# Two-layer transformer block on one core: the layer norm between the last two attentions computed with tokens on partitions, two convolution blocks read where they were accumulated, and the last two token blocks of the output left to VectorE

## The chip, the cores and the metric

The kernel runs on one core of a Trainium2 chip. The core has TensorE (PE in the rows), VectorE (DVE), ScalarE (ACT), GpSimd (POOL), a queue engine that issues transfers (SP), and 16 DMA engines. The metric is the device time of one execution in microseconds (us).

## The reference

x has 512 tokens of 1024 channels. A first block mixes a causal depthwise convolution (width 31) with a dilated window attention and is followed by a feed-forward layer. A second block has two more attentions, and after each of them a residual and a layer norm. The parts that the change touches:

```python
a = a_val * jax.nn.sigmoid(a_gate)
a = causal_depthwise_conv(a, conv_w[l], conv_b[l])
a = jax.nn.silu(rms_norm(a, conv_norm_g[l]))
y_a = a @ w_conv_out[l]
...
def layer_norm(x, g, b):
    mu = jnp.mean(x, axis=-1, keepdims=True)
    var = jnp.mean(jnp.square(x - mu), axis=-1, keepdims=True)
    return (x - mu) * lax.rsqrt(var + LN_EPS) * g + b
...
for i in range(DEPTH_2):                    # i = 0: dsa_mixer, i = 1: stick_breaking_mixer
    y = mixer(x, ...)                       # ends in (o * silu(g)) @ w_out
    x = layer_norm(ALPHA * x + y, ln_g[i], ln_b[i])
```

## The kernel before

Activations lie with channels on partitions: a [1024, 512] matrix is 8 tiles ("blocks", c = 0 to 7) of 128 channels by 512 tokens. Every fp32 product is made of three matmuls on halves of the operands, `hi*hi`, `hi*lo` and `lo*hi` (lines 302 to 304, always in that order); a pair `h, l` of tiles such as `Ah, Al` is such a split, made by ScalarE (`h`) and VectorE (`l`). The class `Weights` loads 512 KB weight blocks (`wraw`, two in flight), ScalarE rounds them to `whi` (line 120) and GpSimd subtracts to get `wlo` (line 124).

TensorE's order is written out by hand: `Stream` holds a list of chunks (one chunk is the three matmuls of one of a product's 8 input blocks), `pe.after(n, fn)` runs `fn` when n more chunks are issued, and `together` takes chunks of several products in turn. The other engines' instructions are put in order by a scheduler.

The places that the change touches:

1. **The convolution's end (stage `mid1`).** Each convolution block is accumulated by VectorE. Six of the eight blocks are done earlier; blocks 6 and 7 (`LATE`) run here, each in a PSUM bank of tag `pt`, while TensorE multiplies by `w_attn_out`. When the last tap is done, ScalarE copies the bank to SBUF (line 834) and squares the copy (line 1016); the sum of squares goes through `ones_d` on TensorE at a fixed place (`pe.pull(YB)`, lines 1031 and 1032), and ScalarE forms `rc` = exp(-0.5 ln) (lines 1034 and 1035, shown as L193 in the rows). VectorE then works on the 8 blocks (lines 1039, 1042, 1045) and also drains the banks of the `w_attn_out` products (line 1025); the products with `w_conv_out` come next and need both.
2. **The layer norm between the two attentions (class `Between`).** The products with `w_out_a` (class `Outward`) come as six whole blocks and two blocks in token halves (`TS`, 256 tokens each). Means and variances are sums over partitions: VectorE and GpSimd add up blocks, `ones_h` and `ones_d` on TensorE sum over partitions, in `middle` (a provisional mean of blocks 0 to 3) and in `stats` (once for each half). `stats` then normalizes 8 blocks with VectorE, GpSimd and ScalarE. Three products of the next layer's gates (`AHEAD`) follow in halves, then the next layer's query block.
3. **The output (class `Last`)** has the tokens on partitions already: `turn` transposes each finished block on TensorE (line 1315) into `pt` banks, ScalarE copies them to `y`, VectorE takes `bn_stats`; `finish` normalizes two token blocks at a time. Token block 1 is done by ScalarE and GpSimd (`APART`), block 3 half by them and half by VectorE, blocks 0 and 2 by VectorE.

## Time and profile before

| | us |
|---|---|
| median of 3 runs (1580.19 to 1585.54) | 1583.32 |
| profiled execution | 1582.75 |
| its span, first to last instruction | 1580.9 |
| TensorE busy | 1519.2 |
| VectorE busy | 1133.5 |
| ScalarE busy | 827.1 |
| GpSimd busy | 767.0 |

The profile is of one execution, 1.85 us longer than its span and 0.57 us under the median. Busy time is a sum over the span; pipelined matmuls overlap, so a busy TensorE isn't one at its peak. In a timeline row the columns are start (us), duration (us), engine, line, operation, output<-input, operand shapes, count, and in brackets the idle time ahead of it and what is taken to have ended it.

### The profile page before, as it was taken

The page shows a single profiled execution, that of the slowest core. Times are in us where ns is not written, and L with a number is a line of the kernel's source. Part 1 is how long each engine was busy: PE and PEld are TensorE (multiplying, and loading weights), DVE is VectorE, ACT ScalarE, POOL GpSimd, SP SyncE. Part 2 cuts the span into 40 slices and gives each one's busy share as a digit, 9 for nine tenths or more (in the row PEclk, how much of TensorE's full clock was granted, in tenths as well). Part 3 has the DMA queues.
Part 4 walks back from the last instruction along what each step waited for, and adds up shares of the span by engine and source line. Part 5 has one row for each costly group of instructions (what it writes and reads, how often), then busy time and mean ns, then how long its engine had stood idle before and what let it go on. Part 6 is the DMA issues. An engine that isn't in the chain of part 4 may idle for free.

```text
span 1580.9 us, 21344 instructions
## 1 busy us (share of the span) xinstructions
PE 1519.2 (96%) x7870; PEld 1290.7 (82%) x7870; DVE 1133.5 (72%) x1867; ACT 827.1 (52%) x1495; POOL 767.0 (49%) x650
## 2 busy tenths in 40 slices
PE   7999999998999999999999989999999789999996
PEld 5888888887878888888888878888887678888885
DVE  8996578777867567627726679988887765777764
ACT  4454678777343443424424344376665445666642
POOL 3687533333735644454454464544552875334324
PEclk9999999999999999999999999999999799999998
DMA  4333321211324333243332342322220313212212
GB/s 142 91 107 93 107 68 41 80 54 54 98 75 119 108 93 89 85 120 94 93 107 87 95 121 68 93 57 78 62 59 14 95 53 94 68 54 81 67 54 80
DMA packets 234604, 130.37 MB, mean 82 GB/s; under 512 B 5206, under 2 KB 232774, under 8 KB 234500
## 3 DMA queue, kind: packets, MB, share of 16 engines
q1 hardware_dynamic: 234356, 128.75, 27.9%
q8 instruction: 62, 1.02, 0.3%
q14 instruction: 42, 0.34, 0.1%
q10 hardware_dynamic: 144, 0.26, 0.0%
HBM read 126.90 MB, written 2.10 MB: 82 GB/s over the span
## 4 chain that ended last, share of the span: by engine, by line
PE 57%; DVE 25%; ACT 8%; issue 4%; POOL 3%; DMA 3%; SPq 0%; DVEq 0%; ACTq 0%; POOLq 0%
PE pj L302 9%; PE pj L303 9%; PE pj L304 9%; DVE pt L832 6%; PE s L303 5%; PE s L302 5%; PE s L304 5%; PE o L513 3%; POOL wlo L124 2%; PE pt L594 2%; PE pj L326 2%; PE pj L328 2%; PE pj L327 2%; PE s L583 1%; DVE score L1445 1%
## 5 line engine op out<-in xcount | busy, mean ns | idle before, releaser
L124 POOL TENSOR_TENSOR wlo<-wraw,whi 128x256 fp32r<-128x256 f32 (+2 forms) x548 | 654.2, 1218 | 698.7 <-ACT whi L120 655.0
L120 ACT CAST whi<-wraw 128x1024 fp32r<-128x1024 f32 (+3 forms) x255 | 243.9, 965 | 243.9 <-PE pj L303 79.0
L302 PE MATMUL pj<-Ah,whi 128*128 128x512 f32 (+3 forms) x896 | 359.5, 401 | 3.7 <-DVE v L719 2.1
L304 PE MATMUL pj<-Ah,wlo 128*128 128x512 f32 (+3 forms) x896 | 348.3, 389 | 2.8 <-POOL wlo L124 2.8
L303 PE MATMUL pj<-Al,whi 128*128 128x512 f32 (+3 forms) x896 | 348.5, 389 | 0.0
L304 PEld LDWEIGHTS pj<-Ah,wlo 128*128 128x128 f32 (+1 forms) x896 | 168.9, 189 | 39.2 <-POOL wlo L124 4.1
L302 PEld LDWEIGHTS pj<-Ah,whi 128*128 128x128 f32 (+1 forms) x896 | 169.5, 189 | 29.1 <-DVE Al L475 1.8
L303 PEld LDWEIGHTS pj<-Al,whi 128*128 128x128 f32 (+1 forms) x896 | 169.6, 189 | 23.9
L832 DVE SCALAR_TENSOR_TENSOR pt<-S,cw,pt 128x494 f32<-128x494 f32 (+26 forms) x210 | 141.8, 733 | 5.5 <-ACT pt L825 3.5
L302 PE MATMUL s<-Ah,whi 128*128 128x512 f32 (+1 forms) x352 | 136.6, 388 | 7.8 <-ACT Ah L1301 4.0
L303 PE MATMUL s<-Al,whi 128*128 128x512 f32 (+1 forms) x352 | 136.3, 387 | 3.7 <-DVE Al L1302 3.7
L304 PE MATMUL s<-Ah,wlo 128*128 128x512 f32 (+1 forms) x352 | 135.9, 386 | 0.0
L326 PE MATMUL pj<-whi,Ah 128*128 128x256 f32 x384 | 112.4, 293 | 1.3 <-DVE q L534 1.3
L597 DVE TENSOR_TENSOR PTl<-pt,PTh 128x512 fp32r<-128x512 f32 x144 | 85.9, 597 | 32.7 <-ACT PTh L596 31.7
L328 PE MATMUL pj<-whi,Al 128*128 128x256 f32 x384 | 108.5, 282 | 0.0
L327 PE MATMUL pj<-wlo,Ah 128*128 128x256 f32 x384 | 108.3, 282 | 0.0
L193 ACT ACTIVATE P<-P,nm 128x128 f32<-128x128 f32 (+3 forms) x128 | 72.0, 563 | 62.9 <-DVE nm L627 61.7
L745 DVE SCALAR_TENSOR_TENSOR u<-ur,fw,u 128x511 f32<-128x511 f32 x44 | 74.9, 1705 | 37.5 <-ACT u L744 37.5
L302 PEld LDWEIGHTS s<-Ah,whi 128*128 128x128 f32 x352 | 68.0, 193 | 21.9 <-ACT Ah L1301 4.6
L596 ACT CAST PTh<-pt 128x512 fp32r<-128x512 f32 x144 | 73.1, 513 | 19.1 <-PE pt L594 18.7
L303 PEld LDWEIGHTS s<-Al,whi 128*128 128x128 f32 x352 | 68.1, 194 | 17.1 <-DVE Al L1302 4.6
L594 PE MATMUL pt<-ident,P 128*128 128x128 f32 x480 | 76.7, 273 | 2.5 <-ACT P L193 0.9
(334 smaller groups left out, 3181.2 us busy)
## 6 DMA issues: line engine op xcount, KB each, us to landing
wraw<-in_w_in_dram SPq DMA_DIRECT2D x56, 512.0 KB
wraw<-in_w_up_dram SPq DMA_DIRECT2D x44, 512.0 KB
wraw<-in_w_in_a_dram SPq DMA_DIRECT2D x36, 512.0 KB
wraw<-in_w_in_b_dram SPq DMA_DIRECT2D x32, 512.0 KB
wraw<-in_w_down_dram SPq DMA_DIRECT2D x16, 512.0 KB
wraw<-in_w_attn_out_dram SPq DMA_DIRECT2D x8, 512.0 KB
wraw<-in_w_conv_out_dram SPq DMA_DIRECT2D x8, 512.0 KB
wraw<-in_w_out_dram SPq DMA_DIRECT2D x8, 512.0 KB
```

Of the source, the lines that this page charges most:

```text
L120: nc.scalar.copy(h, s)
L124: nc.gpsimd.tensor_sub(l[:, k], s[:, k], h[:, k].bitcast(F32))
L302: nc.tensor.matmul(o, hv[:, k, :], ah, start=first, stop=False)
L303: nc.tensor.matmul(o, hv[:, k, :], al, start=False, stop=False)
L304: nc.tensor.matmul(o, lv[:, k, :], ah, start=False, stop=last)
L326: nc.tensor.matmul(o, ah, hv, start=k == 0, stop=False)
L327: nc.tensor.matmul(o, ah, lv, start=False, stop=False)
L328: nc.tensor.matmul(o, al, hv, start=False, stop=k == 7)
L594: nc.tensor.transpose(pt[:, at:at + 128], self.P[r][:, k0:k0 + 128], ident)
L597: nc.vector.tensor_sub(l[:, :at], pt[:, :at], f32(h)[:, :at])
L745: nc.vector.scalar_tensor_tensor(u[:, 1:], v[:, :S - 1], fw[:, 1, j:j + 1], u[:, 1:], op0=OP.mult, op1=OP.add)
L832: nc.vector.scalar_tensor_tensor(o, a, w, o, op0=OP.mult, op1=OP.add)
```

## The change

The convolution blocks 6 and 7 are no longer copied out of PSUM: a dictionary `held` keeps the bank, and the square and the first normalizing step read it there. The loads of ScalarE's function tables around `rc` are written out (`act_tables`). `Between` becomes a second user of the transposing code of `Last` (now the class `Turned`): each finished block of `w_out_a` is transposed, statistics come from `bn_stats`, two token blocks are normalized by VectorE and ScalarE (`finish`), and each channel block is transposed back (`back`) 7 + 2c chunks later, where gain and bias are applied and the halves `h, l` are written. In `Last`, token block 3 is done by VectorE alone, in two pieces of 512 channels with a transfer each.

```diff
-APART = {1: D, 3: 512}
+APART = {1: D}
-STATS = (9, 14)
+BACK = (7, 2)
...
-                    if j == 0:
+                    if j == 0 and self.c in LATE:
+                        held[self.c] = self.acc
+                    elif j == 0:
                         pe.after(2, lambda: nc.scalar.copy(self.a, self.acc))
...
-                    nc.scalar.activation(sq, accs[c], AF.Square)
+                    nc.scalar.activation(sq, held.get(c, accs[c]), AF.Square)
...
+            act_tables(LN_EXP)
             for c in range(ND):
                 pe.add(w_attn_out, 0, 8, 128 * c, oS, yb_done(c))
...
             act(rc, rc, AF.Exp, scale=-0.5)
+            act_tables("exp_and_others")
...
-                nc.vector.scalar_tensor_tensor(t, t, cg_half[:, c:c + 1], rc, op0=OP.mult, op1=OP.mult)
+                nc.vector.scalar_tensor_tensor(t, held.get(c, t), cg_half[:, c:c + 1], rc, op0=OP.mult, op1=OP.mult)
...
-    class Between(Outward):
...
-        def middle(self, h, l):
...
-        def shift(self, c, ts):
...
-        def stats(self, half):
...
-    class Last(Outward):
+    class Turned(Outward):
...
+        def scales(self, ts):
+            rstd = self.rstd[:, ts[0]:ts[-1] + 1]
+            for t in ts:
+                nc.vector.bn_aggr(self.mv[:, t], self.stats[:, t])
+            act(rstd, self.mv[:, ts[0]:ts[-1] + 1, 1], AF.Ln, bias=eps5)
+            act(rstd, rstd, AF.Exp, scale=-0.5)
+
+    class Between(Turned):
+        def finish(self, ts):
+            self.scales(ts)
+            mv, rstd, off = self.mv, self.rstd, self.off
+            for t in ts:
+                nc.vector.scalar_tensor_tensor(off[:, t:t + 1], mv[:, t, 0:1], -1.0, rstd[:, t:t + 1], op0=OP.mult, op1=OP.mult)
+            for k in range(0, D, 512):
+                for t in ts:
+                    z = self.y[:, t, k:k + 512]
+                    if t % 2:
+                        nc.scalar.activation(z, z, AF.Identity, bias=off[:, t:t + 1], scale=rstd[:, t:t + 1])
+                    else:
+                        nc.vector.tensor_scalar(z, z, mv[:, t, 0:1], rstd[:, t:t + 1], op0=OP.subtract, op1=OP.mult)
+            for c in range(ND):
+                pe.after(BACK[0] + BACK[1] * c, lambda c=c: self.back(c, ts))
+
+        def back(self, c, ts):
+            if ts[0] == 0:
+                self.ys.append(act_pair(keep, "A", ND))
+            pt = ps_t()[:, :S // 2]
+            for i, t in enumerate(ts):
+                nc.tensor.transpose(pt[:, 128 * i:128 * i + 128], self.y[:, t, 128 * c:128 * c + 128], ident)
+            h, l = (a[:, 128 * ts[0]:128 * ts[-1] + 128] for a in self.ys[c])
+            g, b = lng[:, c:c + 1], lnb[:, c:c + 1]
+            e = self.pool.tile([128, S // 2], F32, name="e", bufs=3)
+            nc.scalar.activation(h, pt, AF.Identity, bias=b, scale=g)
+            if c % 2:
+                nc.scalar.activation(e, pt, AF.Identity, bias=b, scale=g)
+            else:
+                nc.vector.tensor_scalar(e, pt, g, b, op0=OP.mult, op1=OP.add)
+            nc.vector.tensor_sub(l, e, f32(h))
...
+                step = D if t < NT - 1 else D // 2
+                for a in range(x, D, step):
+                    k = slice(a, a + step)
+                    z = self.y[:, t, k]
+                    nc.vector.scalar_tensor_tensor(z, z, mv[:, t, 0:1], g[:, k], op0=OP.subtract, op1=OP.mult)
+                    nc.vector.scalar_tensor_tensor(z, z, rstd[:, t:t + 1], b[:, k], op0=OP.mult, op1=OP.add)
+                    (nc.scalar if a else nc.sync).dma_start(out[128 * t:128 * t + 128, k], z)
```

On ScalarE, in the convolution's end, the rows before (S_920 and S_1011 are convolution blocks 6 and 7 in SBUF, `pt` their PSUM banks, `th` a square):

```order
L834 COPY S_920<-pt 128x512
L120 CAST whi<-wraw 128x1024
L834 COPY S_1011<-pt 128x512
L1016 ACTIVATE th<-S_920 128x512
L1016 ACTIVATE th<-S_1011 128x512
L1019 CAST sth<-ssum 128x512
L120 CAST whi<-wraw 128x1024
L193 ACT_TABLE_LOAD
L193 ACTIVATE rc<-pt,eps_70 128x512
L193 ACT_TABLE_LOAD
L193 ACTIVATE rc<-rc 128x512
```

And the same place now (line 202 is the written-out load; the lines of the rest have shifted by two or three):

```order
L202 ACT_TABLE_LOAD
L120 CAST whi<-wraw 128x1024 x2
L1016 ACTIVATE th<-pt 128x512
L120 CAST whi<-wraw 128x1024
L1016 ACTIVATE th<-pt 128x512
L1019 CAST sth<-ssum 128x512
L120 CAST whi<-wraw 128x1024
L193 ACTIVATE rc<-pt,eps_70 128x512
L193 ACTIVATE rc<-rc 128x512
L202 ACT_TABLE_LOAD
```

The two copies are gone, one table load stands four roundings ahead of `rc` and the other behind it, with none between `rc`'s two steps.

Further on, VectorE before, up to the first drains of `w_attn_out` banks (line 1025, `tga<-tga,s`):

```order
L1045 SCALAR_TENSOR_TENSOR Al<-S_831,Ah 128x512
L1042 SCALAR_TENSOR_TENSOR S_920<-th,S_920 128x512
L1039 SCALAR_TENSOR_TENSOR S_1011<-S_1011,cg_half,rc 128x512
L1025 SCALAR_TENSOR_TENSOR tga<-tga,s 128x512
L1045 SCALAR_TENSOR_TENSOR Al<-S_920,Ah 128x512
L1042 SCALAR_TENSOR_TENSOR S_1011<-th,S_1011 128x512
L1025 SCALAR_TENSOR_TENSOR tga<-tga,s 128x512
```

And the same place now (S_918 and S_1009 are blocks 6 and 7, lines 1041, 1044 and 1047 the three steps):

```order
L1041 SCALAR_TENSOR_TENSOR S_1009<-pt,cg_half,rc 128x512
L1047 SCALAR_TENSOR_TENSOR Al<-S_829,Ah 128x512
L1047 SCALAR_TENSOR_TENSOR Al<-S_918,Ah 128x512
L1044 SCALAR_TENSOR_TENSOR S_1009<-th,S_1009 128x512
L1025 SCALAR_TENSOR_TENSOR tga<-tga,s 128x512 x2
```

Both drains now stand behind the last block's second step: 23 of VectorE's steps on the 8 blocks are ahead of the first drain, where there were 21. At this place ScalarE had these rows before (`th` is the tanh of a block):

```order
L1044 ACTIVATE Ah<-S_831 128x512
L193 ACTIVATE th<-S_920 128x512
L120 CAST whi<-wraw 128x1024
L1044 ACTIVATE Ah<-S_920 128x512
L193 ACTIVATE th<-S_1011 128x512
```

And it has these now:

```order
L1046 ACTIVATE Ah<-S_829 128x512
L1046 ACTIVATE Ah<-S_918 128x512
L193 ACTIVATE th<-S_1009 128x512
L120 CAST whi<-wraw 128x1024
L1046 ACTIVATE Ah<-S_1009 128x512
```

The rounding of a weight block, which GpSimd's subtraction waits for, stands behind the last `th`, where it stood ahead of it.

In `Between`, ScalarE now (line 1235 copies a transposed block to `y`, `128x4x128` a whole block and `128x2x128` a half; line 1283 normalizes):

```order
L120 CAST whi<-wraw 128x1024 x2
L1235 COPY y<-pt 128x4x128 x2
L120 CAST whi<-wraw 128x1024
L1235 COPY y<-pt 128x4x128 x2
L120 CAST whi<-wraw 128x1024 x2
L1235 COPY y<-pt 128x4x128
L120 CAST whi<-wraw 128x1024
L1235 COPY y<-pt 128x4x128
L1235 COPY y<-pt 128x2x128 x2
L193 ACTIVATE rstd<-mv,eps_71 128x2
L120 CAST whi<-wraw 128x1024
L193 ACTIVATE rstd<-rstd 128x2
```

Behind the last row stand the two steps of line 1283. None of these rows was there before except the `whi` ones: a rounding of a weight block stands ahead of the copy of block 2, and one between the two steps of `rstd`.

TensorE in the same stage, before, around the statistics of the first half (`ogh, ogl` are the attention's output, chunks of block 7's second half):

```order
L304 MATMUL pj<-ogh,wlo 128x256
L1286 MATMUL pt<-sth,ones_d 128x256
L1287 MATMUL pt<-stl,ones_d 128x256
L1286 MATMUL pt<-sth,ones_d 128x256
L1287 MATMUL pt<-stl,ones_d 128x256
L302 MATMUL pj<-ogh,whi 128x256
```

And now, at the first transpose back (line 1294; line 1234 transposes a finished block):

```order
L303 MATMUL pj<-ogh,wlo 128x256
L1294 MATMUL pt<-ident,y 128x128 x2
L301 MATMUL pj<-ogh,whi 128x256
L302 MATMUL pj<-ogl,whi 128x256
L303 MATMUL pj<-ogh,wlo 128x256
L1234 MATMUL pt<-ident,S_10848 128x128 x2
L301 MATMUL pj<-ogh,whi 128x256
```

The four sums over partitions are gone; pairs of transposes stand between chunks instead, and the first pair back stands seven chunks behind the first half's last transpose.

## Rows read from the trace of the kernel before

**Rows 1.** The page: each engine's busy us (share of the span) xinstructions.

```profile
PE 1519.2 (96%) x7870; PEld 1290.7 (82%) x7870; DVE 1133.5 (72%) x1867; ACT 827.1 (52%) x1495; POOL 767.0 (49%) x650
```

**Rows 2.** Three stretches: length, busy time (instructions) of each engine, granted clock, DMA.

```profile
460.00:466.00 6.00, 5.82 (x13) 4.20 (x14) 3.37 (x6) 1.57 (x2) 2.37 (x1) 0.50 0.27 80
1224.00:1287.76 63.76, 49.03 (x287) 44.26 (x287) 51.93 (x75) 24.46 (x45) 49.64 (x53) 0.84 0.23 67
1541.00:1569.00 28.00, 26.53 (x176) 23.47 (x174) 11.12 (x22) 8.55 (x16) 12.28 (x16) 1.00 0.17 53
```

**Rows 3.** Timeline of TensorE at the first product with `w_conv_out`.

```profile
459.92 0.77 PE L302 MATMUL s<-Ah,whi 128*128 128x512 f32 x1 [3.61 <-ACT th L193]
```

**Rows 4.** Timeline of VectorE in the convolution's end.

```profile
439.52 3.40 DVE L1039 SCALAR_TENSOR_TENSOR S<-S,cg_half,rc 128x512 f32<-128x512 f32 x5 [3.61 <-ACT rc L193]
...
444.65 2.90 DVE L1039 SCALAR_TENSOR_TENSOR S<-S,cg_half,rc 128x512 f32<-128x512 f32 x1
447.46 1.88 DVE L1045 SCALAR_TENSOR_TENSOR Al<-S,Ah 128x512 fp32r<-128x512 f32 x3
449.27 4.08 DVE L1042 SCALAR_TENSOR_TENSOR S<-th,S 128x512 f32<-128x512 f32 x3
...
456.35 2.83 DVE L1039 SCALAR_TENSOR_TENSOR S<-S,cg_half,rc 128x512 f32<-128x512 f32 x1
459.10 0.68 DVE L1025 SCALAR_TENSOR_TENSOR tga<-tga,s 128x512 f32<-128x512 f32 x1
```

**Rows 5.** Timeline of ScalarE around `rc`.

```profile
435.56 1.28 ACT L193 ACT_TABLE_LOAD   x1
...
437.56 1.28 ACT L193 ACT_TABLE_LOAD   x1
```

**Rows 6.** Timeline of GpSimd in the convolution's end.

```profile
443.29 3.70 POOL L124 TENSOR_TENSOR wlo<-wraw,whi 128x1024 fp32r<-128x1024 f32 x1 [5.27 <-ACT whi L120]
```

**Rows 7.** Timeline of TensorE in `Between`: longest wait, and the query block's start.

```profile
1250.56 0.58 PE L1286 MATMUL pt<-sth,ones_d 128*128 128x256 f32 x1 [4.66 <-ACT sth L1284]
...
1287.76 0.40 PE L302 MATMUL pj<-Ah,whi 128*128 128x512 f32 x1
```

**Rows 8.** Timeline of TensorE: neighbouring matmuls, and four transposes among them.

```profile
1237.10 0.28 PE L302 MATMUL s<-ogh,whi 128*128 128x256 f32 x1
1237.22 0.28 PE L303 MATMUL s<-ogl,whi 128*128 128x256 f32 x1
...
1541.02 0.39 PE L303 MATMUL pj<-ogl,whi 128*128 128x512 f32 x1
1541.25 0.39 PE L304 MATMUL pj<-ogh,wlo 128*128 128x512 f32 x1
1541.48 0.60 PE L1315 MATMUL pt<-ident,rc 128*128 128x128 f32 x4
...
1542.38 0.39 PE L304 MATMUL pj<-ogh,wlo 128*128 128x512 f32 x1
```

**Rows 9.** Timeline: a weight rounding in `Between`; `Last`'s statistics, wait and copy.

```profile
1227.87 1.04 ACT L120 CAST whi<-wraw 128x1024 fp32r<-128x1024 f32 x1 [2.44 <-POOL wlo L124]
...
1548.61 2.47 DVE L1322 BATCH_NORM_STATS2 stats<-y 128x6 f32<-128x512 f32 x4 [6.86 <-ACT y L1316]
...
1551.82 0.63 PE L1315 MATMUL pt<-ident,e 128*128 128x128 f32 x4 [0.86 <-DVE e L1212]
...
1552.48 0.59 ACT L1316 COPY y<-pt 128x512 f32<-128x512 f32 x1 [2.44 <-PE pt L1315]
```

**Rows 10.** Timeline of `Last`: the last transposes, and ScalarE's normalizing step.

```profile
1568.58 0.41 PE L1315 MATMUL pt<-ident,e 128*128 128x128 f32 x2 [0.61 <-DVE e L1212]
...
1571.22 0.81 ACT L1355 ACTIVATE y<-y,mr,nr 128x512 f32<-128x512 f32 x1
```

**Rows 11.** Line 1301, ScalarE over 256 tokens: xcount, ns min/median/max, first and last start.

```profile
L1301 ACT ACTIVATE Ah<-S,vec x16: 492/508/511, 1257.5 to 1285.2; 128x256 fp32r<-128x256 f32 x16
```

**Rows 12.** Timeline of VectorE at the end of the kernel.

```profile
1570.12 2.78 DVE L1359 SCALAR_TENSOR_TENSOR y<-y,mv,g 128x1024 f32<-128x1024 f32 x1
...
1574.49 2.94 DVE L1360 SCALAR_TENSOR_TENSOR y<-y,rstd,b 128x1024 f32<-128x1024 f32 x2
```

More of the change, by code (lines that the diff above doesn't have):

```diff
@@ L219, in model_kernel @@
     ones_d = const.tile([128, 128], F32R, name="ones_d")
-    ones_h = const.tile([128, 128], F32R, name="ones_h")
     ones_b = const.tile([128, 128], F32R, name="ones_b")
@@ L443, in model_kernel @@
         nc.vector.tensor_scalar(ones_d, zero128, 1.0 / D, None, op0=OP.add)
-        nc.vector.tensor_scalar(ones_h, zero128, 2.0 / D, None, op0=OP.add)
         nc.vector.tensor_scalar(ones_b, zero128, 0.0, None, op0=OP.add)
@@ L809, in model_kernel @@
         o32 = mix1.tile([128, ND, S], F32, name="o32")
-        accs, tga = [], {}
+        accs, tga, held = [], {}, {}
         waiting = {"dve": [], "pool": [], "late": []}
@@ L1326, in summed, with buffers @@
             pe.after(4, turn)
-        def normed(self, pool):
+        def buffers(self, pool):
             self.pool = pool
@@ L1333, in normed @@
             self.rstd = pool.tile([128, NT], F32, name="rstd")
+        def scales(self, ts):
[5 more added lines that the diff above has]
+    class Between(Turned):
+        def normed(self, pool, ys, prods):
+            self.buffers(pool)
+            self.off = pool.tile([128, NT], F32, name="off")
+            self.ys = ys
+            self.run()
+            for half in range(2):
+                pe.together(*[p[half] for p in prods])
+            pe.finish()
+        def finish(self, ts):
[27 more added lines that the diff above has]
+            nc.vector.tensor_sub(l, e, f32(h))
@@ L1334, in normed @@
+    class Last(Turned):
+        def normed(self, pool):
+            self.buffers(pool)
             self.g, self.b = (pool.tile([128, D], F32, name=n) for n in "gb")
@@ L1340, in finish @@
         def finish(self, ts):
-            mv, g, b = self.mv, self.g, self.b
-            rstd = self.rstd[:, ts[0]:ts[-1] + 1]
-            for t in ts:
-                nc.vector.bn_aggr(mv[:, t], self.stats[:, t])
-            act(rstd, mv[:, ts[0]:ts[-1] + 1, 1], AF.Ln, bias=eps5)
-            act(rstd, rstd, AF.Exp, scale=-0.5)
-            rstd = self.rstd
+            self.scales(ts)
+            mv, rstd, g, b = self.mv, self.rstd, self.g, self.b
             for t in ts:
                 x = APART.get(t, 0)
-                y, z = self.y[:, t, :x], self.y[:, t, x:]
+                y = self.y[:, t, :x]
                 if x:
@@ L1357, in finish @@
                     nc.gpsimd.tensor_sub(y, b[:, :x], y)
-                if x < D:
-                    nc.vector.scalar_tensor_tensor(z, z, mv[:, t, 0:1], g[:, x:], op0=OP.subtract, op1=OP.mult)
-                    nc.vector.scalar_tensor_tensor(z, z, rstd[:, t:t + 1], b[:, x:], op0=OP.mult, op1=OP.add)
-                    nc.sync.dma_start(out[128 * t:128 * t + 128, x:], z)
                 if x:
-                    (nc.sync if t < NT - 1 else nc.scalar).dma_start(out[128 * t:128 * t + 128, :x], y)
+                    nc.sync.dma_start(out[128 * t:128 * t + 128, :x], y)
+                step = D if t < NT - 1 else D // 2
[5 more added lines that the diff above has]
+                    (nc.scalar if a else nc.sync).dma_start(out[128 * t:128 * t + 128, k], z)
     W.pieces = PIECES
```

70 lines of the change are left out of this document (removed).

## The prediction

> **What bounds the kernel now.** The page comes first: TensorE is busy 1519 of 1580.9 us [rows 1], so a change can only win where TensorE waits or runs slowly. The table of stages shows where that is. In the 63.8 us between the first four finished blocks of `w_out_a` and the next layer's query block TensorE is busy for 49.0 and the mean granted clock is 0.84 [rows 2]. What the work of that stretch would take follows from the pitch of neighbouring matmuls: 0.228 us for 512 columns, 0.12 for 256 [rows 8]. It holds 12 chunks of whole blocks (36 matmuls), 80 half chunks (240), and ten sums over partitions (2 and 8): 8.2 + 28.8 + 1.4 = 38.4 us. So 25.3 of 63.8 us are lost, 14.7 as waiting (63.8 - 49.0) and 10.6 to the clock and to matmuls that start behind a wait. The longest wait, 4.66 us, is for the sums of the first half [rows 7]; VectorE is busy for 51.9 of the 63.8 us [rows 2] and is what the waits end on.
>
> A second place is the convolution's end. TensorE waits 3.61 us before the first product with `w_conv_out` [rows 3]. The row names ScalarE, but what frees the bank that this product writes is VectorE's drain at 459.10, 0.68 long [rows 4]. Behind the wait 13 matmuls run in 6 us at a granted clock of 0.50, that is 1.2 GHz [rows 2]: 5.8 us of work that takes 3.0 at the full pitch. The third place is the end of the kernel, where VectorE's last step starts at 1574.49 and ends at 1577.43 [rows 12]; the span ends 3.5 us later, with the transfer.
>
> The parts lie in different stages with TensorE saturated between them, so the gains add.
>
> **Part 1, the convolution's end.** The copies out of PSUM cost nothing themselves, since the sums behind them meet TensorE at a fixed place that it reaches on time either way. The two table loads, 1.28 us each, stand between that place and VectorE's first step at 439.52 [rows 4, 5]. Now one is far ahead, beside taps, and the other runs beside VectorE's first step. The two steps of `rc` then follow each other: From the first load's start to VectorE's are 3.96 us, 2.56 of them loads; the sums end some 0.4 us under the first load, so VectorE starts about 2.1 us sooner. From there to the drain it had 21 steps. Alone a step takes 0.63 us (three in 1.88) [rows 4]. Three stretches hold stalls: 2.90 for one step, 4.08 for three, 2.83 for one, so about 2.3 + 2.2 + 2.2 = 6.7 us [rows 4], each while GpSimd runs one undivided `wlo` (the first at 443.29 [rows 6]). Now 23 steps stand ahead of the drain, 1.3 us more, but the third weight rounding stands behind the last `th`, so its subtraction starts when the drains are being issued: 2.2 us less. Drain: 2.1 - 1.3 + 2.2 = 3.0 us sooner, and TensorE's wait falls from 3.6 to 0.6. In `Last` a wait of 0.86 [rows 9] lies in a stretch that is granted 1.00 throughout [rows 2], so I count the slow matmuls as regained for half: 1.5 of 2.8. Sum 4.5 us. Bounds: 1.0 (the third stall stays ahead of the drain, the clock falls as before) and 6.4 (all of 3.6 + 2.8).
>
> The first step of blocks 6 and 7 now has one operand in PSUM. The trace has such steps only as drains, 0.68 us while no subtraction runs [rows 4], so I price it like the others. The Trainium skill ("SBUF — State Buffer", section "Who interferes with whom") says that a VectorE instruction with at most one SBUF input, outside its two-port modes, doesn't contend with GpSimd. The stalled steps above have two SBUF inputs, so the trace agrees that far; the rule would only move the stall to the next step.
>
> **Part 2, the layer norm.** Removed are the ten sums over partitions, 1.4 us of TensorE, and the work that the waits end on: for each half VectorE's shifts, adds and the three passes over 8 blocks. Added are 64 transposes. Four of them widen the distance of two matmuls by 1542.38 - 1541.25 - 3 x 0.228 = 0.445 us [rows 8], so 64 take 7.1. TensorE's work in the stretch becomes 38.4 - 1.4 + 7.1 = 44.1 us, and 19.7 us is the most that can be won. Waits remain at three places:
> - Block 4's transposes stand four chunks behind its last one. ScalarE copies blocks 2 and 3 to `y` only behind a weight rounding that starts at 1227.87 [rows 9], so they are copied by 1227.87 + 1.04 + 2 x 0.59 = 1230.1; four `bn_stats` take 2.47 [rows 9], and block 4's residual step behind them 0.68, which makes 1233.2. TensorE gets there at 1221.3 + 12 chunks x 0.683 + 4 x 0.445 = 1231.3. Wait: 2.0 us. The same place in `Last` waits 0.86 [rows 9], the lower bound.
> - The first transpose back. In `Last` it takes from 1568.58 to 1572.03 (1571.22 + 0.81) from the last transposes to the end of ScalarE's normalizing step over 512 channels [rows 10]; here a weight rounding of 1.04 stands between the two steps of `rstd`, so 4.5. Covered by the transposes (0.22) and seven half chunks (2.5): wait 1.8 us.
> - The same for the second half: no rounding between, but ScalarE has the transposes back in its queue (about 1 us); and three pairs of transposes cover 0.7 more. Wait 1.1 us.
>
> Behind these places a channel block costs ScalarE 0.5 or 1.0 us [rows 11] and VectorE some 0.8 or 0.4 (two or one steps of 256 columns, each a little over half of the 0.68 for 512), against three half chunks (1.08 us) and a pair of transposes (0.22) on TensorE: it stays the bound, also where a subtraction against GpSimd takes twice as long. The waits are 4.9 us. For the clock I take 2 us, as each wait is at most half the 4.66 that opened the slowest stretch. The stretch then lasts 44.1 + 4.9 + 2 = 51.0, a gain of 12.8. Bounds: 18 (waits 1.7, no clock) and 5 (waits twice as long and 5 us of clock). GpSimd loses its adds and subtractions and so delays no weight; weights are loaded by SP in the same order.
>
> **Part 3, the end.** Token block 2's first step ends at 1572.90, stalled by GpSimd on block 1, as it will be. Behind it come one step of 1024 and three of 512 columns with GpSimd idle, 1.3 + 3 x 0.65 (steps alone take 0.63 to 0.68 for 512 [rows 4]): 1576.2 against 1577.43, 1.2 us. The last transfer is of 256 KB before and after. Bounds 0.5 and 1.8. I take 1.1.
>
> **The sum.** 4.5 + 12.8 + 1.1 = 18.4 us off a span of 1580.9, which makes 1562.5; with the 1.85 us around it 1564.4, and since the profiled execution is 0.6 us under the median, the runs should lie at 1564.9.
>
> **Rivals.**
> - **The waits move instead of going.** Copies, scales and weight roundings queue on ScalarE, and each of the three waits in part 2 doubles, with 3 us more of slow clock. For it: two weight roundings stand in front of copies that TensorE needs. Against it: `Last` has the same pattern and waits little. Part 2 gives 12.8 - 4.9 - 3 = 4.9, in all 10.5 us: 1572.8.
> - **Part 1 gives nothing.** VectorE is stalled as often as before, and the two added steps eat most of the 2.1 us. Then 13.9 us: 1569.4.
> - **TensorE's clock stays low among the transposes.** 37 us of products lie in part 2's stretch; at 1.2 GHz they take up to 37 us more. Without any clock cost the sum is 20.4 us, so the kernel is slower by more than the bound below once about 25 of those 37 us are paid, two thirds of the products; if all are, it is slower by 16.6: 1599.9. Against it: in `Last` 32 transposes stand among such products from 1541 to 1569, and the stretch is granted 1.00 [rows 2]. The Trainium skill ("TensorE: Matmul & The Clock Gate", section "Part 4: PE-mode transpose") says that the full clock doesn't engage for transposes, which don't count as busy in the same way; by that rule this rival would be the forecast, and the trace doesn't bear it out where transposes are 32 of 176 matmuls; here they will be 64 of some 340.
> - **No change that can be measured.** Waits as in the first rival, the clock costing 10 us as now (8 more than I took), parts 1 and 3 at their lower bounds: 12.8 - 4.9 - 8 + 1.0 + 0.5 = 1.4 us, 1581.9.
>
> **Chances.** Forecast 0.62; waits move 0.18; part 1 nothing 0.10; no change 0.06; slow clock 0.04. A difference of 0.3%, 4.7 us, is about what a measurement of this kernel can tell from none. So faster 0.90, same 0.06, slower 0.04. The range goes from part 2's and part 1's better bounds together (1583.3 - 18 - 6.4 - 1.1 = 1557.8) to a little over the first rival: 1558 to 1575.
>
> **What the changed profile would show.** Part 1: no table load between the sums and `rc`, the first step of line 1041 near 437.4, TensorE's first wait on `w_conv_out` under 1.5 us. Part 2: about 51 us from block 4's fifth chunk to the query block, three waits of 1 to 2 us at lines 1234 and 1294, a granted clock above 0.9 over it. Part 3: VectorE's last step ends 3.5 us ahead of the span's end as now, with GpSimd idle since block 1. The prediction is wrong if TensorE waits for weights (line 124), if a granted clock of 0.5 holds over tens of us, or if a wait in part 2 is as long as the 4.66 us of now.

## The result and the profile of the changed kernel

Measured together, the kernel before has a median of 1583.10 us and the changed one 1563.15 us (four runs each). The ratio is 0.9872 with a 95% interval of 0.9852 to 0.9891: 20.3 us faster, 17.3 to 23.4. Forecast were 18.4 us and 1564.9.

The page, engines (to be read beside [rows 1]):

```profile
PE 1516.5 (97%) x7924; PEld 1290.6 (83%) x7924; DVE 1106.4 (71%) x1845; ACT 827.5 (53%) x1494; POOL 742.5 (48%) x635
```

TensorE's busy time hardly moves, 1519.2 to 1516.5, while 19.2 us leave the span (1580.9 to 1561.7): 16.5 of them were waiting. Busy time also holds matmuls at a slow clock, and these became fewer, as the windows show. By windows, with the columns of [rows 2]: the kernel before, from the last chunk of its first four blocks of `w_out_a` (at 1221.28) to the query block:

```profile
1221.28:1287.76 66.48, 51.75 (x299) 46.32 (x298) 54.62 (x79) 24.46 (x45) 52.36 (x55) 0.85 0.22 64
```

The changed kernel, by windows too: the six us behind the first product with `w_conv_out`, and the stretch from the same chunk to the query block:

```profile
457.24:463.24 6.00, 6.00 (x26) 4.96 (x27) 3.35 (x4) 0.86 (x1) 4.42 (x2) 1.00 0.40 110
1216.78:1270.06 53.28, 49.30 (x353) 46.04 (x352) 29.14 (x56) 26.91 (x49) 34.25 (x43) 0.97 0.28 80
```

The layer norm's stretch is 13.2 us shorter though it holds some 54 more matmul instructions, and VectorE's load in it falls from 54.6 to 29.1. Behind the convolution's end 26 matmuls run in six us at a granted clock of 1.00, where there were 13 at 0.50.

Timeline of TensorE now: its waits in the three places, and the query block's start.

```profile
457.24 0.47 PE L301 MATMUL s<-Ah,whi 128*128 128x512 f32 x1 [0.21 <-ACT Ah L1046]
...
1227.62 0.63 PE L1234 MATMUL pt<-ident,S 128*128 128x128 f32 x4 [0.68 <-DVE S L1214]
...
1243.51 0.51 PE L1294 MATMUL pt<-ident,y 128*128 128x128 f32 x2 [1.93 <-ACT y L1283]
...
1253.30 0.28 PE L303 MATMUL s<-Ah,wlo 128*128 128x256 f32 x1
1254.64 0.78 PE L1294 MATMUL pt<-ident,y 128*128 128x128 f32 x2 [1.07 <-DVE y L1285]
...
1270.06 0.40 PE L301 MATMUL pj<-Ah,whi 128*128 128x512 f32 x1
```

The 3.61 us of [rows 3] are 0.21, the 4.66 of [rows 7] are gone, and the three waits that the prediction named are 0.68, 1.93 and 1.07 us (forecast 2.0, 1.8, 1.1). A fourth, of 0.19 us, lies between the last two.

Timeline of VectorE in the convolution's end:

```profile
438.03 2.40 DVE L1041 SCALAR_TENSOR_TENSOR S<-S,cg_half,rc 128x512 f32<-128x512 f32 x3 [1.75 <-ACT rc L193]
...
443.37 2.90 DVE L1041 SCALAR_TENSOR_TENSOR S<-S,cg_half,rc 128x512 f32<-128x512 f32 x1
...
449.92 0.74 DVE L1041 SCALAR_TENSOR_TENSOR S<-pt,cg_half,rc 128x512 f32<-128x512 f32 x1
450.59 2.24 DVE L1047 SCALAR_TENSOR_TENSOR Al<-S,Ah 128x512 fp32r<-128x512 f32 x1
...
456.42 1.27 DVE L1025 SCALAR_TENSOR_TENSOR tga<-tga,s 128x512 f32<-128x512 f32 x2
```

And of GpSimd at the same place:

```profile
449.83 2.44 POOL L124 TENSOR_TENSOR wlo<-wraw,whi 128x1024 fp32r<-128x1024 f32 x1 [4.12 <-ACT whi L120]
456.44 5.23 POOL L124 TENSOR_TENSOR wlo<-wraw,whi 128x1024 fp32r<-128x1024 f32 x2 [4.17 <-ACT whi L120]
```

The step at 449.92, block 6's first, has one operand in PSUM and takes 0.74 us although GpSimd's subtraction began 0.09 us before it. The next one has both in SBUF and is held up: it ends at 450.59 + 2.24 = 452.83, 0.56 us behind the end of that subtraction (449.83 + 2.44 = 452.27). The third subtraction (456.44) now starts 0.02 us behind the first drain (456.42). Both are as the prediction had them. The Trainium skill ("SBUF — State Buffer", section "Who interferes with whom") says that a VectorE instruction with at most one SBUF input, outside its two-port modes, doesn't contend with GpSimd; the trace agrees, 0.74 us beside a subtraction where block 7's first step took 2.83 with two [rows 4].

Timeline of ScalarE around the first half's `rstd`, where the rounding of a weight block lies between the two steps:

```profile
1240.30 0.29 ACT L193 ACTIVATE rstd<-mv,eps 128x2 f32<-128x2 f32 x1 [0.83 <-DVE mv L1257]
1240.55 1.05 ACT L120 CAST whi<-wraw 128x1024 fp32r<-128x1024 f32 x1
1241.51 0.20 ACT L193 ACTIVATE rstd<-rstd 128x2 f32<-128x2 f32 x1
1242.58 1.53 ACT L1283 ACTIVATE y<-y,off,rstd 128x512 f32<-128x512 f32 x2 [0.88 <-DVE off L1278]
```

Timeline of VectorE at the end (against [rows 12]):

```profile
1551.98 3.45 DVE L1333 SCALAR_TENSOR_TENSOR y<-y,mv,g 128x1024 f32<-128x1024 f32 x2
1555.35 1.94 DVE L1334 SCALAR_TENSOR_TENSOR y<-y,rstd,b 128x1024 f32<-128x1024 f32 x2
1557.21 0.74 DVE L1333 SCALAR_TENSOR_TENSOR y<-y,mv,g 128x512 f32<-128x512 f32 x1
1557.99 0.75 DVE L1334 SCALAR_TENSOR_TENSOR y<-y,rstd,b 128x512 f32<-128x512 f32 x1
```

VectorE ends 8.30 us behind the start of the last transposes (1550.44), where it took 8.85 before, and the span ends 3.0 us later in place of 3.5.

### The profile page after: what moved, and what is told of

Its sections match the earlier page's. It is cut to its first block, busy times and chain, and to the rows that moved or that the text cites. A ratio compares the mean times of both kernels' runs of the same rounds, so it can differ in the third digit from the quotient of the medians.

```text
span 1561.7 us, 21424 instructions
## 1 busy us (share of the span) xinstructions
PE 1516.5 (97%) x7924; PEld 1290.6 (83%) x7924; DVE 1106.4 (71%) x1845; ACT 827.5 (53%) x1494; POOL 742.5 (48%) x635
## 3 DMA queue, kind: packets, MB, share of 16 engines
q1 hardware_dynamic: 234356, 128.75, 28.3%
## 4 chain that ended last, share of the span: by engine, by line
PE 63%; DVE 23%; ACT 7%; issue 4%; DMA 2%; POOL 1%; SPq 0%; ACTq 0%; DVEq 0%; POOLq 0%
PE pj L301 11%; PE pj L302 10%; PE pj L303 10%; DVE pt L830 6%; PE s L301 6%; PE s L302 6%; PE s L303 6%; PE o L511 3%; PE pt L592 2%; PE pj L325 2%; PE pj L327 2%; PE pj L326 2%; ACT k L557 1%; PE s L581 1%; DVE score L1417 1%
## 5 line engine op out<-in xcount | busy, mean ns | idle before, releaser
L124 POOL TENSOR_TENSOR wlo<-wraw,whi 128x256 fp32r<-128x256 f32 (+2 forms) x548 | 645.7, 1204 | 705.8 <-ACT whi L120 655.5
```

Source lines behind the costliest of these rows:

```text
L124: nc.gpsimd.tensor_sub(l[:, k], s[:, k], h[:, k].bitcast(F32))
```

## The experiments

All ratios are to the kernel before, with 95% intervals. "First" is the time from the first sum through `ones_d` to the first product with `w_conv_out`. "Stage" is the time from the end of the first four blocks' last chunk (in the kernels with transposes, from the first transpose of `Between`, which stands there) to the query block; it is left out where `Between` is that of the kernel before. Both are read from the timeline of the one execution of each kernel that was profiled.

| run | median us | ratio | first us | stage us |
|---|---|---|---|---|
| before | 1583.1 | 1 | 24.9 | 65.8 |
| changed | 1563.15 | 0.9872 (0.9852 to 0.9891) | 21.3 | 52.6 |
| tables alone | 1578.10 | 0.9972 (0.9961 to 0.9983) | 22.3 | |
| PSUM alone | 1580.54 | 0.9985 (0.9976 to 0.9994) | 22.0 | |
| Between alone | 1567.32 | 0.9903 (0.9888 to 0.9918) | 24.9 | 51.1 |
| end alone | 1582.45 | 0.9996 (0.9986 to 1.0005) | 25.1 | |
| statistics deferred | 1559.79 | 0.9849 (0.9837 to 0.9862) | 21.2 | 51.2 |
| rounding held | 1558.36 | 0.9845 (0.9833 to 0.9858) | 21.4 | 50.2 |
| back later | 1562.11 | 0.9867 (0.9853 to 0.9880) | 21.4 | 52.6 |
| both moves | 1557.42 | 0.9836 (0.9823 to 0.9848) | 21.1 | 49.2 |
| four transposes | 1564.47 | 0.9881 (0.9868 to 0.9895) | 20.9 | 57.2 |
| in pieces (one execution) | 1560.24 | | 23.8 | 49.3 |
| second half later | 1555.96 | 0.9826 (0.9810 to 0.9842) | 21.3 | 47.4 |
| same, copies back | 1558.86 | 0.9836 (0.9819 to 0.9854) | 22.3 | 47.6 |

### The table loads alone

```diff
+            act_tables(LN_EXP)
             for c in range(ND):
                 pe.add(w_attn_out, 0, 8, 128 * c, oS, yb_done(c))
...
             act(rc, rc, AF.Exp, scale=-0.5)
+            act_tables("exp_and_others")
```

> The kernel before with the two written-out table loads alone; the copies out of PSUM stay. Theory A (the prediction's mechanism: the loads leave the path to VectorE's first step, and the third weight rounding falls behind the last th, so that its subtraction runs behind the first drain): TensorE's 3.6 us wait at the first product with w_conv_out falls to about 0.2 to 0.6, no slow clock follows it, and the kernel is 6 to 7 us faster, ratio 0.9955 to 0.9965. Rival B (it is the reading in PSUM that does it: two copies less on ScalarE, and first steps that GpSimd doesn't hold up): the loads alone take about 2 us off the wait, 1.5 us stay, the clock falls all the same; 2 us faster, ratio 0.9985 to 0.999.

4.4 us faster (2.7 to 6.2). Timeline of TensorE in this run:

```profile
457.38 0.47 PE L302 MATMUL s<-Ah,whi 128*128 128x512 f32 x1 [1.00 <-ACT Ah L1046]
```

And the six us from there, by windows:

```profile
457.38:463.38 6.00, 6.00 (x26) 4.96 (x27) 3.33 (x4) 0.86 (x1) 4.39 (x2) 1.00 0.37 107
```

The first product comes 2.6 us sooner behind the sums and waits 1.00 us; behind it 26 matmuls run in six us at 1.00, where 13 did at 0.50. From the first sum to the 27th matmul of these products, where both kernels run at the full pitch again, it takes 28.3 us in place of 34.2: 5.9 us, most of the 6.9 that the whole change wins by the same measure (27.3). The order of ScalarE's rows at this place is that of the whole change but for the two copies. Rival B falls: its 1.5 us of wait and slow clock aren't there. Theory A was a little high: it had 6 to 7 us and a wait of 0.2 to 0.6.

### Reading in PSUM alone

```diff
+                    if j == 0 and self.c in LATE:
+                        held[self.c] = self.acc
-                    if j == 0:
+                    elif j == 0:
                         pe.after(2, lambda: nc.scalar.copy(self.a, self.acc))
```

and the two uses of `held.get(c, ...)`.

> The kernel before with blocks 6 and 7 read in their PSUM banks alone; the table loads stay where they were. Theory A: nothing measurable, ratio 0.999 to 1.001; the 3.6 us wait stays within 0.5 us, and the 6 us at a granted clock of 0.50 behind it too, since the sums meet TensorE at a fixed place and the third subtraction still runs ahead of the drain. Rival B: the wait falls by 2 us or more, 4 to 5 us faster, ratio 0.997.

2.4 us faster (0.9 to 3.8): theory A's "nothing" is wrong, and rival B's 4 to 5 us are too much. Timeline of VectorE in this run:

```profile
453.07 0.73 DVE L1041 SCALAR_TENSOR_TENSOR S<-pt,cg_half,rc 128x512 f32<-128x512 f32 x1
453.73 0.67 DVE L1027 SCALAR_TENSOR_TENSOR tga<-tga,s 128x512 f32<-128x512 f32 x1
454.33 1.61 DVE L1047 SCALAR_TENSOR_TENSOR Al<-S,Ah 128x512 fp32r<-128x512 f32 x1
...
456.46 0.67 DVE L1027 SCALAR_TENSOR_TENSOR tga<-tga,s 128x512 f32<-128x512 f32 x1
```

Of GpSimd:

```profile
452.49 2.90 POOL L124 TENSOR_TENSOR wlo<-wraw,whi 128x1024 fp32r<-128x1024 f32 x1 [3.56 <-ACT whi L120]
```

And of TensorE, its two waits:

```profile
454.55 0.47 PE L302 MATMUL s<-Ah,whi 128*128 128x512 f32 x1 [0.95 <-ACT th L193]
...
457.28 0.77 PE L302 MATMUL s<-Ah,whi 128*128 128x512 f32 x1 [1.80 <-ACT Ah L1046]
```

The third subtraction still starts ahead of the drain, but block 7's first step reads PSUM and isn't held up (0.73 us, where [rows 4] has 2.83), nor is the drain. The stall comes one step later, at 454.33, ahead of the second drain, and TensorE waits there instead: 2.75 us in all, in place of 3.61. So each edit takes the third stall off the path to the first drain in its own way, and they overlap: from the first sum to the 27th matmul 5.9 and 2.8 us are won alone (31.5 us here), 6.9 together. The runs with neither edit, `Between` alone and the end alone, have the kernel before's time there (34.2 and 34.1).

### Between alone

The convolution's end and `Last`'s `finish` are those of the kernel before.

> The kernel before with the new Between alone; the convolution's end and the output are as before. Theory A (the parts add): 13 us faster, ratio 0.9915 to 0.992, with waits of about 0.7, 1.9 and 1.1 us at block 4's transposes and at the first transposes back of the two halves, and one stretch of about 3.4 us at 0.50 granted behind the second. Rival C (part of the stage's gain hangs on the convolution's end, by way of when weights are loaded or of the clock): 10 us or less, ratio above 0.9935.

15.4 us faster (13.0 to 17.8), somewhat more than theory A's 13. The three waits are 0.67, 1.93 and 1.06 us, as in the whole change, but the stage is 51.1 and not 52.6 us. What differs is the clock behind the same wait of 1.93, here by windows (the column ahead of the last two is the granted clock); the changed kernel:

```profile
1243.51:1247.01 3.50, 3.50 (x17) 3.50 (x18) 2.62 (x5) 2.31 (x5) 1.31 (x2) 0.52 0.18 44
```

And this run:

```profile
1246.24:1249.74 3.50, 3.50 (x30) 3.50 (x31) 3.15 (x7) 3.28 (x7) 1.32 (x2) 1.00 0.19 48
```

17 matmuls against 30 in the same 3.5 us: the 1.5 us are the clock's, and they are there in the one execution and not in the other. Rival C falls.

### The end alone

```diff
-APART = {1: D, 3: 512}
+APART = {1: D}
```

with the new loop over two pieces in `Last`.

> The kernel before with the last two token blocks on VectorE alone as the only edit. Theory A: about 1.1 us faster, ratio 0.9990 to 0.9997, less than the timing can tell from nothing; in the profile the span ends 11.2 us behind the last transposes in place of 12.3. Rival D (the last transfer hides it: its landing, not VectorE's last step, sets the end): the distance stays 12.3 within 0.3.

0.6 us faster (2.2 faster to 0.8 slower), which the timing can't tell from nothing. The profile shows it: from the last transposes to the span's end 11.2 us in place of 12.3, VectorE done after 8.3. Rival D falls.

### Statistics behind block 4's residual step

```diff
-                    for t in range(a, b):
-                        src = pt[:, 128 * t:128 * t + 128] if c == ND - 1 else self.y[:, t, 128 * x:128 * y]
-                        nc.vector.bn_stats(self.stats[:, t, i, :], src)
+                    def stats(order=None):
+                        for t in range(a, b):
+                            src = pt[:, 128 * t:128 * t + 128] if c == ND - 1 else self.y[:, t, 128 * x:128 * y]
+                            ins = nc.vector.bn_stats(self.stats[:, t, i, :], src).ins
+                            if order:
+                                tc.add_manual_dep(ins, self.added.name, no_sync)
+                    if c == self.OPENED - 1:
+                        pe.after(6, lambda: stats(True))
+                    else:
+                        stats()
```

`added` is the last residual step, here block 4's.

> The changed kernel with one thing moved in Between and in Last: VectorE's four bn_stats of the first four blocks stand behind block 4's residual step, where they stood ahead of it. Theory A (block 4's transposes wait for a residual step that is ready 2 us earlier but queued behind the four bn_stats): the waits of 0.68 and 0.85 us at block 4's transposes in Between and in Last go, nothing takes their place, about 1.6 us faster than the changed kernel, ratio 0.986. Rival B (the four bn_stats are late in turn and hold up block 5's transposes or the first half's scales): no gain.

The waits at block 4's transposes are gone in both stages and nothing takes their place; the stage is 1.4 us shorter and the way from the query block to the last transposes 1.1 (280.4 to 279.2). Some 0.6 of the 1.4 come only behind the wait of 1.93, which is there as before: the granted clock behind it is 0.67 over 3.5 us here and 0.52 in the changed kernel. By medians 3.4 us, by ratio 3.6 with an uncertainty of some 3.7, which alone would not tell the move from nothing. The waits are as theory A has them.

### The rounding behind `rstd`

```diff
             self.off = pool.tile([128, NT], F32, name="off")
+            W.limit = [b[0] is w_in_b for b in W.blocks].index(True) + AHEAD - 1
...
-            self.scales(ts)
+            exp = self.scales(ts)
+            if W.limit:
+                W.limit, W.behind = None, exp
+                W.ahead()
```

`Weights` rounds no block past `limit`, and its next rounding is ordered behind `behind`, the second step of `rstd`. On ScalarE the two rows change places, and nothing else does.

> The changed kernel with one thing moved: the rounding of the third gate block stands behind the second step of the first half's rstd on ScalarE, where it stood between the two steps. Theory A (the rounding's 1.04 us lie on the path to the first transpose back): that wait falls from 1.93 to about 0.9 us and the slow clock behind it, if it comes at all, with it; 1.0 to 2.5 us faster than the changed kernel, ratio 0.9855 to 0.9865. Rival B (the third gate block's subtraction, which takes 3.1 us, is then late and TensorE waits for it at the first gate products): no gain.

Timeline of TensorE in this run:

```profile
1241.69 0.33 PE L1303 MATMUL pt<-ident,y 128*128 128x128 f32 x1 [0.54 <-ACT y L1292]
```

The wait falls from 1.93 to 0.54 and no slow clock follows; the second half's grows from 1.07 to 1.54. The stage is 2.4 us shorter, within the 1.0 to 2.5 of theory A; the ratio's 4.3 us, with an uncertainty of some 3.7, is above it. Of the 2.4 us 1.5 are the clock's: against the 51.1 us of `Between` alone, which has the wait of 1.93 without the slow clock, 0.9 are left. No wait for the third gate block's halves appears, so rival B falls.

### Transposes back three half chunks later

```diff
-BACK = (7, 2)
+BACK = (10, 2)
```

> The changed kernel with each transpose back three half chunks later (ten behind its half's last transposes in place of seven). Theory A (what the half chunks cover counts): both waits shrink by 3 x 0.36 us, from 1.93 to 0.85 and from 1.07 to 0, about 2 us faster than the changed kernel. Rival B (the wait only moves: the first gate product needs block 0's halves, which end some 2 us behind its transposes back, and now has one chunk between them instead of four): the first half gains nothing, TensorE waits 1 us or more at the first gate chunk or at the third matmul of it, in all 0 to 1 us faster.

Timeline of TensorE in this run:

```profile
1240.73 0.41 PE L1294 MATMUL pt<-ident,y 128*128 128x128 f32 x2 [0.66 <-ACT y L1283]
...
1244.11 0.58 PE L302 MATMUL s<-Al,whi 128*128 128x256 f32 x1 [1.64 <-DVE Al L1303]
```

Rival B holds: the wait moves from the transposes to the first gate chunk, which needs block 0's halves, and the stage stays at 52.6 us. Behind the wait of 1.64 the granted clock is 0.51 over 3.5 us.

### Both moves

> The changed kernel with the two moves of the runs before together: bn_stats of the first four blocks behind block 4's residual step, and the rounding behind rstd. Theory A: the gains add, 2.6 to 4 us faster than the changed kernel, about 1559.5 to 1560.5, ratio to the kernel before 0.9845 to 0.9855. Rival B: what one wait gives up the next takes; within 1 us of the changed kernel.

The stage is 49.2 us, 3.4 less than in the changed kernel, and `Last` keeps its 1.1: 4.5 us by the profile, 5.7 by the ratios with an uncertainty of some 3.7. The gains add, 3.4 against 1.4 + 2.4 but for the clock behind the 1.93 us, which both runs count. Theory A's 2.6 to 4 us were a little low, and rival B falls. 1.5 of the 4.5 us are that slow clock; against the stage of `Between` alone it is 1.9 + 1.1.

### Every transpose back four times

The later ones write what is there already. Base: both moves.

```diff
-                nc.tensor.transpose(pt[:, 128 * i:128 * i + 128], self.y[:, t, 128 * c:128 * c + 128], ident)
+                for _ in range(4):
+                    nc.tensor.transpose(pt[:, 128 * i:128 * i + 128], self.y[:, t, 128 * c:128 * c + 128], ident)
```

> The version with both moves (e8), with each of the 32 transposes back issued four times into the same place, so 96 more among the same 77 chunks. Theory A (a transpose costs TensorE its own time and nothing else): 96 x 0.111 = 10.7 us at most, 96 x 0.06 = 5.8 at least if they follow each other closer in a row of eight; less what the waits at the transposes back (0.5 and 1.5 us) take up; 5 to 10 us slower than e8, and the granted clock over the stretch stays at 0.95 or more. Rival B (transposes don't count as work for the clock, and these outnumber the matmuls around them): the granted clock falls to 0.5 among them for 10 us or more, and the stretch grows by 15 to 30 us.

Timeline of TensorE at one channel block:

```profile
1242.07 0.28 PE L308 MATMUL pj<-ogh,wlo 128*128 128x256 f32 x1
1242.19 1.03 PE L1312 MATMUL pt<-ident,y 128*128 128x128 f32 x8
1242.98 0.36 PE L306 MATMUL pj<-ogh,whi 128*128 128x256 f32 x1
```

And by windows, over the stretch of the transposes back:

```profile
1239.00:1275.00 36.00, 35.65 (x304) 35.02 (x303) 18.35 (x40) 20.16 (x37) 18.80 (x22) 1.00 0.12 36
```

The run is 7.0 us slower than both moves by medians. The stage grows by 8.0 us, and 1.9 us of waits (0.54 and 1.53, now 0.21) are filled too: 9.9 / 96 = 0.10 us for each, close to the 0.111 of the prediction. 128 of the 304 matmuls in these 36 us are transposes, and the granted clock is 1.00 throughout. Rival B falls, and with it the prediction's rival of the slow clock. The Trainium skill ("TensorE: Matmul & The Clock Gate", section "Part 4: PE-mode transpose") says that transposes don't engage the full clock; the trace, granted 1.00 among them, disagrees for transposes with matmuls between. A stretch of transposes alone was not tried.

### Subtractions in pieces

`W.pieces` stays 4 through the convolution's end. Base: both moves.

> The version with both moves (e8), with GpSimd's eleven subtractions that are issued in the convolution's end made in four pieces of 256 columns each in place of one of 1024. Theory A (a VectorE step with two operands in SBUF is held up until GpSimd's running instruction ends): no step on the 8 blocks takes longer than 1.5 us, where single ones took 2.2 to 2.9, but several are held up in a row; the 23 steps together take the same within 1 us, and the kernel's time doesn't change. Rival B (the hold-up is by GpSimd's whole work, however cut): single steps of 2 us or more stay.

Timeline of VectorE in this run:

```profile
444.58 1.24 DVE L1045 SCALAR_TENSOR_TENSOR S<-S,cg_half,rc 128x512 f32<-128x512 f32 x1
445.75 1.23 DVE L1051 SCALAR_TENSOR_TENSOR Al<-S,Ah 128x512 fp32r<-128x512 f32 x1
446.89 1.22 DVE L1045 SCALAR_TENSOR_TENSOR S<-S,cg_half,rc 128x512 f32<-128x512 f32 x1
```

And of GpSimd:

```profile
444.54 4.17 POOL L128 TENSOR_TENSOR wlo<-wraw,whi 128x256 fp32r<-128x256 f32 x4 [3.43 <-ACT whi L121]
```

One stall of 2.3 us becomes four of about 0.55, and from VectorE's first step to the first drain it is 18.5 us (18.3 in the run with both moves, 18.4 in the changed kernel): theory A for VectorE. Its "time doesn't change" is wrong: GpSimd takes 3.7 to 4.3 us for a block in place of 2.4, the next weight block is late, its rounding stands ahead of `rc` on ScalarE, and VectorE's first step starts 3.3 us behind the second sum's start in place of 1.8. TensorE waits 1.69 us. One execution is too few to compare its time.

### The second half's transposes five half chunks later

```diff
-                pe.after(BACK[0] + BACK[1] * c, lambda c=c: self.back(c, ts))
+                pe.after(BACK[0] + LAG * (ts[0] > 0) + BACK[1] * c, lambda c=c: self.back(c, ts))
```

`LAG` is 5. Base: both moves.

> The version with both moves (e8), with the second half's transposes back five half chunks later (twelve behind its last transposes in place of seven); the first half's stay. Theory A (24 chunks of the first half's gate products lie there, so nothing needs them sooner): the wait of 1.53 us at the second half's first transposes back goes and none takes its place; 1.0 to 1.6 us faster than e8, 1556 us, ratio to the kernel before 0.982 to 0.983. Rival B (the wait is not for these but for ScalarE's and VectorE's queues as a whole, which are full in this stretch): a wait of 1 us or more appears at a later transpose back or at the second half's first gate chunk, no gain.

The stage is 1.8 us shorter and the wait of 1.53 gone, but this is given back 13 us behind the query block's start, at a place that neither theory named. Timeline of TensorE there:

```profile
1277.83 0.36 PE L331 MATMUL pj<-whi,Ah 128*128 128x256 f32 x1 [2.06 <-DVE q L538]
```

And of ScalarE:

```profile
1274.12 1.05 ACT L122 CAST whi<-wraw 128x1024 fp32r<-128x1024 f32 x1 [3.70 <-DMA wraw<-in_w_in_b_dram]
```

ScalarE's step for `q` stands behind a rounding that waits for its transfer. In the run with both moves TensorE waits 0.32 us at this place, that rounding starts at 1273.10, GpSimd's next subtraction at 1266.64 and not at 1267.75: GpSimd first adds the halves of the new blocks (line 1215), which are ready later. That the late subtraction makes the transfer late is read from the order of these rows and was not tested by a run of its own. From the query block to the last transposes it takes 1.3 us longer (280.5 and 279.3). By the spans nothing is won (1555.9 and 1556.5), and the medians, 1557.42 and 1555.96, can't tell.

### The same with the copies out of PSUM

> The version with all three moves (e11), with the convolution's blocks 6 and 7 copied out of PSUM again as in the kernel before; the table loads stay written out. Theory A (both edits of the convolution's end take the same third stall off the path to the first drain, so the second one adds little): TensorE's wait at the first product with w_conv_out is 1.0 us in place of 0.2, no slow clock follows, 0.8 to 1.2 us slower than e11, about what the timing can't tell from nothing. Rival B (what the reading in PSUM gave alone, 2.4 us, comes on top): a wait of 2 us or more, 2.4 us or more slower than e11.

The first product waits 1.00 us in place of 0.25 and comes 1.0 us later behind the sums (22.3 and 21.3); no slow clock. By medians 2.9 us slower, by ratio 1.6 with an uncertainty of some 3.7. So beside the tables the reading in PSUM is worth about 1 us by the profile, as theory A has it; the timing alone can't tell it from rival B's 2.4. Here and with the tables alone block 6's first step lasts 2.9 us beside the subtraction, where the changed kernel does that step in 0.74 and only the next one is held up.

## Why the prediction was right, and where it was off

**The mechanism** held in all three parts, and so did additivity: alone they measure 4.4 + 2.4 + 15.4 + 0.6 = 22.8 us, of which some 1.8 count twice (5.9 + 2.8 against 6.9), against 20.3 together, within the intervals. In the profiled execution the parts are worth 6.9, 13.2 and 1.1 us, 21.2 together, and 0.4 were won behind the query block. The span shrinks by 19.2: 1.5 us were lost near 940 us, in code that is the same (below), and 1.0 ahead of the convolution's sums. There two runs with that code unchanged (`Between` alone, the end alone) begin the sums 1.8 and 2.4 us sooner than the kernel before, so 1.0 is within what executions differ by.

**Part 1: 6.9 us, forecast 4.5, upper bound 6.4.** VectorE's start (2.3 us sooner behind the second sum, forecast 2.1) and the third subtraction were right. The first product comes 3.64 us sooner behind the sums, forecast 3.0: the tables alone bring 2.6, and the reading in PSUM, which was priced at nothing ("I price it like the others"), another 1.0. The mis-sized term is "I count the slow matmuls as regained for half: 1.5 of 2.8". All of them are, 6.9 - 3.64 = 3.3 us, since they also go on a little beyond the six us: no run in which TensorE waits 1.0 us or less in all at this place has a slow clock behind it, and all three with 3.6 have six us at 0.50 to 0.52.

**Part 2: 13.2 us, forecast 12.8, in part by errors that cancel.** The price of a transpose (0.111) holds. The waits are 3.7 us in place of 4.9; the one at block 4 was forecast at 2.0 because I let the weight rounding ahead of the copies start 4.5 us sooner along with everything else, at 1223.4, and it started at 1222.36. The clock, forecast at 2 us, costs 1.5 in this execution and nothing in another. Work, waits and clock make 44.1 + 3.7 + 1.5 = 49.3 us, but the stretch of [rows 2] now lasts 50.6 (53.28 less the four chunks, 2.73, ahead of it). For the other 1.3 the sum had no term: neighbouring matmuls overlap, so a wait costs more than the idle time that its row shows (the matmul ahead of the transposes at 1254.64 starts at 1253.30, 1.34 us sooner in place of 0.12, with 1.07 idle), and there is the fourth wait. That VectorE's `bn_stats`, the rounding between `rstd`'s steps and the cover of seven half chunks make these waits was tested by moving each: the first two are causes, the third isn't by itself, since the gate products wait for the same data.

**Part 3: 1.1 us, forecast 1.1, by errors that cancel.** "One step of 1024 and three of 512 columns" miscounts: two pieces have four steps, so VectorE gains 0.55 us and not 1.2. (The row at 1574.49 in [rows 12] is two steps, not the last one alone; the sum only uses its end.) The other 0.5 is the end of the last transfer, 3.0 us behind VectorE in place of the 3.5 that were to stay. It is now issued by ScalarE's queue and was by SP's; that this is why was not tested.

**The rivals.** The waits did not double; part 1 gave more, not nothing; the clock did not stay low among transposes, not even among 128 of them.

## What to carry to other kernels

Ask of each wait what stands ahead of the late instruction in its engine's queue: two moves of rows that were not late themselves (four `bn_stats`, one rounding) won another 4.5 us by the profile, 1.5 of them a slow clock behind a wait, while giving the wait more cover only moved it. A later consumer can make the weights late one stage on, so follow a gain to the next place where the engine waits. And compare kernels stage by stage, from one place in the program to another: two executions of equal code differ by more than many edits are worth.

## What the runs showed of the hardware that was not expected

**A short wait costs the clock in some executions only.** Behind 3.6 us of waiting the granted clock was 0.50 to 0.52 for six us in three runs of three. Behind 1.93 us it was, over 3.5 us, 0.52 in the changed kernel, 0.67 in the run with statistics deferred and 1.00 in the run with `Between` alone; behind 1.64 in the run with transposes back later it was 0.51, behind 1.69 in the run with pieces 1.00. Each is one execution of its own kernel. But the same happens in code that no edit touches: near 940 us TensorE waits for ScalarE twice in the kernel before (1.86 and 2.30 us) and in the changed one (1.85 and 1.43), and the granted clock differs (over 925 to 955 us it is 1.00 in three of the fourteen traces, 0.94 in ten and 0.89 in the changed kernel's). By windows, the changed kernel:

```profile
935.00:945.00 10.00, 8.50 (x25) 6.28 (x26) 7.94 (x12) 4.27 (x9) 2.78 (x4) 0.66 0.36 101
```

And the kernel before:

```profile
939.00:949.00 10.00, 5.84 (x24) 4.32 (x24) 9.52 (x15) 5.76 (x10) 3.79 (x5) 1.00 0.38 105
```

**Cutting GpSimd's instruction in four doesn't shorten the hold-up.** Four subtractions of 256 columns cost VectorE what one of 1024 does (four stalls of about 0.55 us, one of 2.3), and GpSimd 1.3 to 1.9 us more (3.7 to 4.3 in place of 2.4).
